# Plain fp32 products instead of three split ones, and value rows summed on VectorE, in a two-stream encoder with gathered experts

## The chip, the cores and the metric

The kernel runs on one core of one Trainium2 chip. The metric is the device time of one launch in microseconds (us): the median of the runs. Beside it stands one profiled execution, whose trace gives every number below that is not a median.

## The reference, cut to what matters

Two requests (`prompt` and `sample`, 256 tokens of 1024 values each) go through the same two layers. Layer 0 mixes tokens by attention, layer 1 by a gated convolution. Each is followed by a retrieval mixer (PEER): per token, 8 heads choose 16 of 16384 experts each, so 128 rows of the table `u` and 128 rows of the table `v`, 4 KB a row.

```python
def peer_block(xc):                      # 128 tokens
    q = (xc @ w_query).reshape(C, 8, 2, 128)
    s = einsum('chpk,hpnk->chpn', q, sub_keys)
    sv, si = top_k(s, 16)                # two lists of 16 keys
    cand = sv[..., 0, :, None] + sv[..., 1, None, :]
    fv, fi = top_k(cand, 16)             # 16 experts of the pairs
    eidx = ...;  g = softmax(fv)
    h = gelu(einsum('chkd,cd->chk', u_tab[eidx], xc))
    return einsum('chk,chkd->cd', g * h, v_tab[eidx])

for i in range(2):
    h = attention(x) if i == 0 else short_conv(x)
    x = layer_norm(ALPHA * x + h, ...)
    x = layer_norm(ALPHA * x + peer(x), ...)
    x = x + sigmoid(x @ ple_w_gate[i]) * (p[i] @ ple_w_proj[i])
```

All inputs are fp32.

## The kernel before, in words

The two requests are two interleaved streams. Stream A (`thread_a`, request 0) does the retrieval sparsely: it gathers the chosen rows. Stream B (`thread_b`, request 1) does it densely: it multiplies all 16384 rows of both tables, two blocks of 128 experts at a time, and weights them with a scattered matrix `G` that is zero where an expert was not chosen. So A's retrieval lives on DMA, GpSimd (POOL) and VectorE (DVE), and B's on TensorE (PE). Each stream is a generator that yields a cost; the next piece is taken from the stream that is behind, and a priority per stage (`pri`) enters the scheduler, which fixes every engine's order at build time. An engine then runs its list strictly in that order.

The stages of A in layer 0: `attention`, layer norm, `route` (the queries and the two top-16 searches, eight rounds of 4 x 128 scores), `peer_gather`, then `ple` (the gated embedding). In layer 1 `conv` stands for `attention`. Stream B has the same stages with `dense_pre` (8 of the 64 pairs of `u` blocks, run ahead into `pre`) and `peer_dense` for the gather.

**Split products.** A weight tile of 128 x 1024 fp32 (512 KB) is loaded by `wload` on SP's queue into `raw` or `ur`; ScalarE (ACT) writes its rounded part `hi`/`uh` as fp32r (L92), and DVE or POOL the rest `lo`/`ul` (L93; `cycle` deals them out in turn). The moving side (`xh`, `xl`, `bx1T0`, `bx1T1`, `ch`, `cl`) is split too. `mm` and `mm_` then issue three fp32r products for each one: high by high, high by low, low by high (L108 to L110, L114 to L117). Only a few matrices go unsplit as plain fp32: the embedding projection (`e.nat`, L106), the scores and values of the attention (L271 to L273, L297), the key scores (L391).

**Gather.** For token tile `t` (of two) `up` gathers the 128 `u` rows of each token one column of indices at a time: one indirect DMA on POOL's queue brings 128 rows, one per token (L486), and one DVE instruction multiplies it with `x[t]` and sums it up (L505). `down` gathers `v` rows by expert position instead: 128 rows of one token sit on 128 partitions, and a stationary matrix `dg` of 128 x 32 that holds coefficients in one column sums them for one token into `av` (L535). Both share the ring `g` of GB = 5 tiles of 512 KB. The order is: all `u` rows of t = 0, then (with `ORDK`) the `v` rows of t = 0 while B routes, then t = 1. A's next stage, `ple`, begins when both tiles are summed and normed.

**Dense.** For a pair of blocks PE runs `dense_u` (2 x 8 products of 256 columns into `hid`), two scatter groups (L638), and `down` (2 x 4 products of 512 columns into the four `out` banks) for the pair before. A pair needs four weight tiles.

Of the kernel before, what the change touches and what calls it, by code (L numbers as in the profile page):

```python
# [11 lines left out]
F32R = mybir.dt.float32r  # L12
# [30 lines left out]
GB = 5  # L43
UR = 4
US = 2
# [3 lines left out]
def encoder_trunk(ctx: ExitStack, tc: tile.TileContext, A: dict):  # L49
# [62 lines left out]
    def mm_(out, a, b, q, first, last):  # L112
        if q == 0:
            nc.tensor.matmul(out, a[0], b[0], start=first, stop=False)  # L114
            nc.tensor.matmul(out, a[0], b[1], start=False, stop=False)  # L115
        else:
            nc.tensor.matmul(out, a[1], b[0], start=False, stop=last)  # L117

    def at(ops, *ix):
        return tuple(o[(slice(None),) + ix] for o in ops)  # L120

    def wblocks(e, name, nb, cols=512):
        kpb = WB // cols
        src = A[name]
        for b in range(src.shape[1]):
            w = wload(e, src[nb, b])
            yield b * kpb, kpb, tuple(z.rearrange("p (c n) -> p c n", n=cols) for z in w)

    def token_major_steps(e, xt, name, nb, ps, kcs=KC):
        ps += [e.mm() for _ in range(NT)]  # L130
        for c0, n, w in wblocks(e, name, nb):
            for t in range(NT):
                for c in range(n):
                    kc = c0 + c
                    mm(ps[t], at(xt, kc, slice(t * P, (t + 1) * P)), at(w, c), kc == 0, kc == kcs - 1)
            yield 2.5
# [7 lines left out]
    def col_major(e, xt, name, cb):  # L144
        ps = e.mm()[:, :S]
        for c0, n, w in wblocks(e, name, cb, cols=P):
            for kc in range(KC):
                mm(ps, at(w, kc), at(xt, kc), kc == 0, kc == KC - 1)
        return ps

    def transpose_x(e, x, xt, natural=False):
        for t in range(NT):
            for half in range(2):
# [4 lines left out]
                if not natural:  # L158
                    o = at(xt, slice(half * 4, half * 4 + 4), slice(t * P, (t + 1) * P))
                    nc.scalar.activation(o[0], pt, AF.Copy)  # L160
                    if len(o) == 2:
                        nc.vector.tensor_sub(o[1], pt, o[0].bitcast(F32))
                else:
                    for j in range(4):
                        o = tuple(z[:, half * 4 + j].rearrange("p (q a b) -> p b a q", q=16, a=4, b=4)[:, 2 * t:2 * t + 2] for z in xt)
                        s = pt[:, j].rearrange("p (b a q) -> p b a q", b=2, a=4, q=16)
                        nc.scalar.activation(o[0], s, AF.Copy)
                        if len(o) == 2:
                            nc.vector.tensor_sub(o[1], s, o[0].bitcast(F32))
# [43 lines left out]
    def attention(e, g, x):  # L213
# [3 lines left out]
        for kb in range(0, KC, 2):  # L217
            raw = e.k2([2 * S])
            nc.scalar.dma_start(raw, A[f"xT{g}"][:, kb * S:(kb + 2) * S])
            split(*(z[:, kb:kb + 2].rearrange("p c s -> p (c s)") for z in xt), raw)  # L220
# [44 lines left out]
        def attend(hp):  # L265
# [20 lines left out]
            def values(hh, t, pr):  # L286
# [11 lines left out]
                nc.scalar.activation(ot[0][:, h, sl], ov[:, :P], AF.Copy)  # L298
                nc.vector.tensor_sub(ot[1][:, h, sl], ov[:, :P], ot[0][:, h, sl].bitcast(F32))
# [34 lines left out]
    def conv(e, x):  # L334
# [10 lines left out]
        for m in range(KC):  # L345
# [17 lines left out]
            else:  # L363
                nc.vector.tensor_mul(cv, cv, ps)
                nc.scalar.activation(po(ht[0][:, m]), nat(cv), AF.Copy)
                nc.vector.tensor_sub(po(ht[1][:, m]), nat(cv), po(ht[0][:, m]).bitcast(F32))
            yield 10
        if bounce:
            ht = e.xt()
            for kb in range(0, KC, 4):  # L370
                raw = e.raw()
                nc.sync.dma_start(raw, hd[:, kb:kb + 4].rearrange("p c s -> p (c s)"))
                split(*(z[:, kb:kb + 4].rearrange("p c s -> p (c s)") for z in ht), raw)
# [3 lines left out]
    def route(e, i, xt, need_t):  # L377
# [73 lines left out]
        if not need_t:  # L451
            eT = T(stp, [P, NT, P], "eT", I32)
            for t in range(NT):
                pt = e.tr([P])
                nc.tensor.transpose(pt, efs[t], ident)
                nc.vector.tensor_copy(eT[:, t], pt)
            return eis, gts, eT
# [31 lines left out]
    def peer_gather(i, x, sel, done):  # L489
        u, v = A[f"u{i}"], A[f"v{i}"]  # L490
        eis, gts, eT = sel
        cT = T(stp, [P, NT, P], "cT")
        cfs = [T(sp, [P, PH, TOPK], "cf", bufs=2) for _ in range(NT)]

        def up(t, heads):
            pri[0] = PG
            ph[0] = True
            yield 0.0
            cf = cfs[t]
            for h in heads:  # L500
                dots = T(sp, [P, TOPK], "dots", bufs=2)
                for k in range(TOPK):
                    c = h * TOPK + k
                    r = gather(u, eis[t][c // 32][:, c % 32:c % 32 + 1])
                    nc.vector.scalar_tensor_tensor(r, r, 1.0, x[t], op0=ALU.mult, op1=ALU.mult, accum_out=dots[:, k:k + 1])  # L505
                    if k % 4 == 3:
                        yield GCOST
                nc.scalar.activation(cf[:, h], dots, AF.Gelu)
                nc.vector.tensor_mul(cf[:, h], cf[:, h], gts[t][:, h])
# [510 lines left out]
```

## Time and profile before

| | us |
|---|---|
| median of 3 runs (4182.75 to 4189.85) | 4186.15 |
| span of the profiled execution, first to last instruction | 4165.6 |
| median less span: the start and end of a launch around it | 20.5 |
| PE busy in the span | 3705.3 (89%) |
| DVE busy | 2680.9 (64%) |
| POOL busy | 2320.6 (56%) |
| ACT busy | 1521.8 (37%) |
| moved by DMA | 1008.36 MB, mean 242 GB/s |

The span is the time from the first to the last instruction of the program on the core; the launch adds some 20 us around it. Busy times overlap, and a share over the whole span is a mean of stages with different limits, so the stages are read one by one. A matmul's duration in the trace includes its way through the array; what a stream of them costs is the distance from start to start.

### The profile page before, as it was taken

What the parts mean: (1) busy time and instruction counts of PE and PEld (TensorE: products, weight loads), DVE (VectorE), ACT (ScalarE), POOL (GpSimd) and SP (SyncE); (2) the same over time, 40 slices, a digit from 0 to 9 for tenths busy, and PEclk for the clock granted to TensorE, in tenths of its full rate; (3) what the DMA queues carried; (4) which work ended last, traced back from release to release, by engine and by line L of the source; (5) the groups of instructions that cost most, each with busy time, mean ns of one, the idle gap of its engine ahead of it and who ended that gap; (6) DMA issues with size and microseconds to landing.
All of it is one profiled execution on the core that took longest, in us unless ns stands there. A gap on an engine that the chain in (4) does not pass through costs nothing. (4 is left out here: it accounts for less than half of the span.)

```text
span 4165.6 us, 61081 instructions
## 1 busy us (share of the span) xinstructions
PE 3705.3 (89%) x22328; PEld 2720.2 (65%) x22328; DVE 2680.9 (64%) x6741; ACT 1521.8 (37%) x2495; POOL 2320.6 (56%) x1927
## 2 busy tenths in 40 slices
PE   8988776899998889999999975769899888999999
PEld 7876564555357776555579864656466777766756
DVE  2348999758459884222255699989843999833325
ACT  4554443434133333222254543234233333433324
POOL 5436777755557665444411255757555776755550
PEclk9999887999999999999999997789999999999999
DMA  6446777876768887666646567777768888877874
GB/s 208 155 133 214 241 258 267 290 266 237 237 231 286 276 281 240 220 215 212 211 147 194 181 228 259 273 272 267 264 231 279 290 291 292 301 267 266 299 248 154
DMA packets 280525, 1008.36 MB, mean 242 GB/s; under 512 B 31648, under 2 KB 33056, under 8 KB 280224
## 3 DMA queue, kind: packets, MB, share of 16 engines
q0 software_dynamic: 147456, 536.94, 36.9%
q1 hardware_dynamic: 124128, 448.85, 32.6%
q10 hardware_dynamic: 8640, 18.68, 1.3%
q8 instruction: 175, 2.87, 0.3%
q14 instruction: 126, 1.03, 0.1%
HBM read 999.09 MB, written 5.24 MB: 241 GB/s over the span
## 5 line engine op out<-in xcount | busy, mean ns | idle before, releaser
L93 POOL TENSOR_TENSOR ul<-ur,uh 128x1024 fp32r<-128x1024 f32 x299 | 747.9, 2501 | 460.3 <-ACT uh L92 435.5
L92 ACT ACTIVATE uh<-ur 128x1024 fp32r<-128x1024 f32 x592 | 625.3, 1056 | 863.3 <-PE hid L109 402.2
L486 POOL DMA_INDIRECT g<-in_v_dram,eT x512 | 515.7, 1007 | 634.0 <-PE av L535 542.3
L486 POOL DMA_INDIRECT g<-in_u_dram,ei x512 | 646.5, 1263 | 367.4 <-DVE g L505 169.4
L505 DVE SCALAR_TENSOR_TENSOR g<-g,xa 128x1024 f32<-128x1024 f32 x512 | 737.1, 1448 | 17.3 <-DMA g<-in_u_dram,ei 17.3
L535 PE MATMUL av<-g,dg 128*32 128x512 f32 x2048 | 713.8, 606 | 27.8 <-POOL dg L529 16.9
L93 DVE TENSOR_TENSOR ul<-ur,uh 128x1024 fp32r<-128x1024 f32 x293 | 371.2, 1267 | 457.8 <-ACT uh L92 436.2
L110 PE MATMUL hid<-bx1T,ul 128*128 128x256 f32 x1792 | 535.0, 299 | 31.0 <-POOL ul L93 24.0
L108 PE MATMUL hid<-bx1T,uh 128*128 128x256 f32 x1792 | 529.6, 296 | 17.8 <-DVE G L640 11.4
L109 PE MATMUL hid<-bx1T,uh 128*128 128x256 f32 x1792 | 521.7, 291 | 0.0
L110 PEld LDWEIGHTS hid<-bx1T,ul 128*128 128x128 f32 x1792 | 355.0, 198 | 79.4 <-issue 37.4
L115 PE MATMUL out<-ul,ch 128*128 128x512 f32 x1024 | 348.9, 413 | 58.7 <-POOL ul L93 38.1
L108 PEld LDWEIGHTS hid<-bx1T,uh 128*128 128x128 f32 x1792 | 355.4, 198 | 50.1 <-ACT uh L92 21.3
L93 DVE TENSOR_TENSOR cl<-hs,ch 128x256 fp32r<-128x256 f32 x224 | 193.2, 865 | 301.9 <-PE out L117 280.3
L535 PEld LDWEIGHTS av<-g,dg 128*32 128x32 f32 x2048 | 140.7, 109 | 351.2 <-issue 264.4
L109 PEld LDWEIGHTS hid<-bx1T,uh 128*128 128x128 f32 x1792 | 354.1, 198 | 12.7 <-issue 10.3
L437 DVE SCALAR_TENSOR_TENSOR junk<-iota,fif,ci 128x54 f32<-128x54 f32 x1024 | 340.3, 376 | 3.0 <-ACT fif L431 2.0
L109 PE MATMUL mm<-lo,xh 128*128 128x512 f32 x640 | 271.1, 424 | 65.9 <-POOL lo L93 36.2
L117 PE MATMUL out<-uh,cl 128*128 128x512 f32 x1024 | 323.0, 396 | 0.4 <-DVE cl L93 0.4
L93 POOL TENSOR_TENSOR lo<-raw,hi 128x1024 fp32r<-128x1024 f32 x88 | 215.4, 2447 | 165.9 <-ACT hi L92 164.0
L114 PE MATMUL out<-uh,ch 128*128 128x512 f32 x1024 | 302.8, 403 | 5.4 <-ACT uh L92 3.2
L638 PE MATMUL hid<-I,J 128*128 128x32 f16 x3584 | 262.6, 232 | 30.8 <-DVE G L640 29.6
(254 smaller groups left out, 6791.8 us busy)
## 6 DMA issues: line engine op xcount, KB each, us to landing
ur<-in_uT_dram SPq DMA_DIRECT2D x256, 512.0 KB, 4.7
ur<-in_v_dram SPq DMA_DIRECT2D x256, 512.0 KB, 4.3
raw<-in_w_qkv_dram SPq DMA_DIRECT2D x144, 512.0 KB, 4.1
raw<-in_w_q_dram SPq DMA_DIRECT2D x32, 512.0 KB, 3.7
ur<-in_w_q_dram SPq DMA_DIRECT2D x32, 512.0 KB, 4.9
raw<-in_c_in_dram SPq DMA_DIRECT2D x24, 512.0 KB, 4.0
ur<-in_c_in_dram SPq DMA_DIRECT2D x24, 512.0 KB, 4.5
raw<-in_w_out_dram SPq DMA_DIRECT2D x16, 512.0 KB, 3.9
```

Source lines behind the costliest of these rows:

```text
L92: nc.scalar.activation(dst_hi, src, AF.Copy)
L93: (eng or nc.vector).tensor_tensor(dst_lo, src, dst_hi.bitcast(F32), op=ALU.subtract)
L108: nc.tensor.matmul(out, a[0], b[0], start=first, stop=False)
L109: nc.tensor.matmul(out, a[0], b[1], start=False, stop=False)
L110: nc.tensor.matmul(out, a[1], b[0], start=False, stop=last)
L114: nc.tensor.matmul(out, a[0], b[0], start=first, stop=False)
L115: nc.tensor.matmul(out, a[0], b[1], start=False, stop=False)
L117: nc.tensor.matmul(out, a[1], b[0], start=False, stop=last)
L437: lk.scalar_tensor_tensor(junk, iota, fif[:, h, k:k + 1], ci[:, h], op0=ALU.is_equal, op1=ALU.mult, accum_out=ef[:, h * TOPK + k:h * TOPK ...
L486: nc.gpsimd.indirect_dma_start(out=t, out_offset=None, in_=tab, in_offset=bass.IndirectOffsetOnAxis(ap=idx, axis=0))
L505: nc.vector.scalar_tensor_tensor(r, r, 1.0, x[t], op0=ALU.mult, op1=ALU.mult, accum_out=dots[:, k:k + 1])
L535: nc.tensor.matmul(acc[n][g * 32:(g + 1) * 32, :], dg[:, g, ri], rows[g][:, n * 512:(n + 1) * 512], start=r == 0, stop=r == 31)
```

## The change

Every product is one plain fp32 matmul straight from the loaded tile: the splits, their `hi` and `lo` rings, the engines that made them and the second halves of the moving tiles are gone. The `v` rows of stream A are gathered like the `u` rows, one index column at a time with one row per token, and DVE multiplies each row by its coefficient and adds it to `acc` (one instruction per gather, the first one a plain multiplication). The heads run one after the other: the `u` rows of head n + 1, then the `v` rows of head n. The rings grow with the room that is free: GB 5 to 8, `ur` 4 to 5, `raw` 3 to 8 in the attention and 2 to 4 behind it.

```diff
-GB = 5
-UR = 4
-US = 2
+GB = 8
+UR = 5
     def wload(e, src, n=WB):
         raw = e.raw()[:, :n]
         nc.sync.dma_start(raw, src)
-        if not e.split:
-            return (raw,)
-        hi, lo = e.hi()[:, :n], e.lo()[:, :n]
-        split(hi, lo, raw, e.sub())
-        return hi, lo
+        return raw
 
     def mm(out, a, b, first, last):
-        if len(a) == 1:
-            nc.tensor.matmul(out, a[0], b[0], start=first, stop=last)
-        else:
-            nc.tensor.matmul(out, a[0], b[0], start=first, stop=False)
-            nc.tensor.matmul(out, a[0], b[1], start=False, stop=False)
-            nc.tensor.matmul(out, a[1], b[0], start=False, stop=last)
+        nc.tensor.matmul(out, a, b, start=first, stop=last)
...
-            for rb in range(32 // RB):
-                dg = T(sp, [P, 4, RB, 32], "dg", bufs=1)
-                nc.gpsimd.memset(dg, 0.0)
-                nc.gpsimd.tensor_copy(dg..., cg[:, :, rb * RB:(rb + 1) * RB])
-                for ri in range(RB):
-                    r = rb * RB + ri
-                    rows = [gather(v, eT[:, t, g * 32 + r:g * 32 + r + 1]) for g in range(4)]
-                    for n in range(2):
-                        for g in range(4):
-                            nc.tensor.matmul(acc[n][g * 32:(g + 1) * 32, :], dg[:, g, ri], rows[g][:, n * 512:(n + 1) * 512], start=r == 0, stop=r == 31)
...
+        def down(t, h):
+            cf = cfs.pop((t, h))
+            if h == 0:
+                acc[t] = T(stp, [P, D], "acc")
+            for k in range(TOPK):
+                r = gather(v, index(t, h * TOPK + k))
+                c = cf[:, k:k + 1]
+                if h == 0 and k == 0:
+                    nc.vector.tensor_scalar(acc[t], r, c, None, op0=ALU.mult)
+                else:
+                    nc.vector.scalar_tensor_tensor(acc[t], r, c, acc[t], op0=ALU.mult, op1=ALU.add)
+                if k % 4 == 3:
+                    yield GCOST
+            if h == PH - 1:
+                nc.vector.scalar_tensor_tensor(x[t], x[t], ALPHA, acc[t], op0=ALU.mult, op1=ALU.add)
+                done(t)
+
+        cfs, acc = {}, {}
+        yield 0.0
+        steps = [(t, h) for t in range(NT) for h in range(PH)]
+        yield from up(*steps[0])
+        for n, step in enumerate(steps):
+            if n + 1 < len(steps):
+                yield from up(*steps[n + 1])
+            yield from down(*step)
...
-                w = wload(e.un if native else e.v, A[f"v{i}"][blk * P:(blk + 1) * P, :])
...
+                w = wload(e, A[f"v{i}"][blk * P:(blk + 1) * P, :])
                 for t in range(NT):
-                    for q in range(1 if native else 2):
...
+                    for n in range(2):
+                        mm(out[t][n], hs[:, b, t * P:(t + 1) * P], w[:, n * 512:(n + 1) * 512], blk == 0, blk == nblk - 1)
...
-    R1 = 3
+    R1 = 8
...
-        w = p2.enter_context(tc.tile_pool(name="w2", bufs=2))
+        w = p2.enter_context(tc.tile_pool(name="w2", bufs=4))
```

PE's list, in the dense retrieval of layer 1 (rows of the kernel before; `hid` is the sum over a pair of `u` blocks, `uh` and `ul` the halves of a `u` tile, `bx1T` the two halves of B's transposed tokens):

```order
19967 L110 MATMUL hid_32473<-bx1T_5023_24763,ul_32477 128x256
19968 L108 MATMUL hid_32473<-bx1T_5023_24763,uh_32476 128x256
19969 L109 MATMUL hid_32473<-bx1T_5024_24764,uh_32476 128x256
19970 L110 MATMUL hid_32473<-bx1T_5023_24763,ul_32477 128x256
19971 L108 MATMUL hid_32473<-bx1T_5023_24763,uh_32476 128x256
19972 L109 MATMUL hid_32473<-bx1T_5024_24764,uh_32476 128x256
```

And PE's list of the change in the dense retrieval of layer 0, where A's gather ends (`out` are the four banks of B's sum, `xa` A's tokens, which `ple` transposes, `ur` the tile as loaded):

```order
3143 L95 MATMUL out_6254<-ur_8811,hs_8808 128x512
3144 L95 MATMUL out_6251<-ur_8817,hs_8808 128x512
3145 L95 MATMUL out_6252<-ur_8817,hs_8808 128x512
3146 L95 MATMUL out_6253<-ur_8817,hs_8808 128x512
3147 L95 MATMUL out_6254<-ur_8817,hs_8808 128x512
3148 L132 MATMUL av_10474<-ident_75,xa_6_99 128x128 x4
3149 L132 MATMUL av_10480<-ident_75,xa_6_99 128x128
3150 L95 MATMUL hid_8787<-bx1T_4352,ur_8788 128x256 x8
3151 L95 MATMUL hid_8787<-bx1T_4352,ur_8798 128x256 x8
```

Three instructions per product have become one, and A's transposes, which read the finished sum of the gather, stand in PE's list after a fifth of the dense pairs of layer 0; the pairs behind them come later in the list. In layer 1 the same transposes of `xa_6` stand at row 7857 of 11572, ahead of all 56 pairs of `u` blocks that are not run ahead.

DVE's list in the gather stage of layer 0, t = 1, before (`ul` and `cl` are low halves) and in the change:

```order
1605 L505 SCALAR_TENSOR_TENSOR g_11665,dots_11661<-g_11665,xa_6_99 128x1024
1606 L93 TENSOR_TENSOR cl_12636<-hs_12626,ch_12635 128x256
1607 L505 SCALAR_TENSOR_TENSOR g_11668,dots_11661<-g_11668,xa_6_99 128x1024
1608 L93 TENSOR_TENSOR cl_12658<-hs_12626,ch_12657 128x256
1609 L640 TENSOR_TENSOR G_12484<-G_12484,hid_12677 128x16x16
1610 L626 TENSOR_TENSOR I_2864_13025<-I_2863_13024,gT_9233 128x1024
1611 L505 SCALAR_TENSOR_TENSOR g_11671,dots_11661<-g_11671,xa_6_99 128x1024
```

```order
1611 L458 SCALAR_TENSOR_TENSOR g_9608,dots_9409<-g_9608,xa_6_99 128x1024
1612 L458 SCALAR_TENSOR_TENSOR g_9611,dots_9409<-g_9611,xa_6_99 128x1024
1613 L521 SCALAR_TENSOR_TENSOR hs_7752<-hs_7752,G_6959 128x512
1614 L476 SCALAR_TENSOR_TENSOR acc_7706<-g_9617,cf_9199,acc_7706 128x1024
1615 L463 TENSOR_TENSOR cf_9614<-cf_9614,gate_390_1481 128x16
1616 L476 SCALAR_TENSOR_TENSOR acc_7706<-g_9620,cf_9199,acc_7706 128x1024
1617 L551 TENSOR_TENSOR I_2051_7870<-I_2050_7869,gT_6214 128x1024
1618 L565 TENSOR_TENSOR G_7658<-G_7658,hid_7665 128x16x16
```

The low halves are gone from DVE, and rows of `v` (L476, each adding to the `acc` of the one before) stand between those of `u` (L458).

## Rows read from the trace of the kernel before

**Rows 1.** The page: the span, and the busy time of each engine.

```profile
span 4165.6 us, 61081 instructions
PE 3705.3 (89%) x22328; PEld 2720.2 (65%) x22328; DVE 2680.9 (64%) x6741; ACT 1521.8 (37%) x2495; POOL 2320.6 (56%) x1927
```

**Rows 2.** The busy time of each engine by stage. Columns: the stretch in us from the start, its length, busy us and instructions of each engine, the granted share of PE's clock, the mean busy share of the DMA engines, GB/s.

```profile
0.00:292.00 292.00, 275.15 (x1344) 227.88 (x1344) 91.05 (x118) 156.81 (x230) 135.54 (x141) 0.99 0.51 168
303.00:816.00 513.00, 386.71 (x1812) 313.21 (x1811) 461.72 (x1388) 213.55 (x369) 386.31 (x349) 0.86 0.73 249
816.00:1043.00 227.00, 216.52 (x1125) 126.74 (x1125) 149.53 (x966) 79.30 (x172) 120.18 (x148) 0.98 0.74 258
1043.00:1571.00 528.00, 465.15 (x3344) 346.70 (x3340) 388.77 (x565) 164.47 (x263) 332.53 (x229) 0.95 0.77 264
1571.00:2097.00 526.00, 522.33 (x2692) 294.37 (x2691) 136.68 (x198) 134.09 (x193) 232.74 (x187) 1.00 0.64 214
...
2522.00:2969.00 447.00, 326.60 (x1840) 255.60 (x1841) 430.89 (x1680) 155.78 (x304) 288.67 (x285) 0.86 0.77 267
...
3214.00:3616.00 402.00, 353.89 (x2596) 301.09 (x2595) 373.46 (x485) 153.30 (x236) 297.01 (x177) 0.98 0.84 293
3616.00:4093.00 477.00, 474.38 (x2944) 322.96 (x2942) 171.81 (x225) 164.14 (x234) 259.25 (x196) 1.00 0.78 265
4093.00:4166.00 73.00, 63.43 (x245) 44.94 (x243) 39.79 (x49) 24.71 (x37) 0.00 (x0) 0.97 0.42 148
```

**Rows 3.** Instructions of single lines with the first and the last start: L211 is the residual add at the end of a mixer (`xa` stream A, `y` and `G` stream B), L539 the one behind A's gather, L670 the one behind B's dense retrieval.

```profile
L211 DVE SCALAR_TENSOR_TENSOR xa<-xa,mm x4: 672/683/687, 279.3 to 291.9; 128x512 f32<-128x512 f32 x4
L211 DVE SCALAR_TENSOR_TENSOR y<-y,mm x4: 671/679/685, 798.9 to 816.2; 128x512 f32<-128x512 f32 x4
L539 DVE SCALAR_TENSOR_TENSOR xa<-xa,av x8: 686/687/689, 1212.7 to 4069.1; 128x512 f32<-128x512 f32 x8
L670 DVE SCALAR_TENSOR_TENSOR G<-G,out x8: 666/676/680, 2522.0 to 4095.3; 128x512 f32<-128x512 f32 x8
```

**Rows 4.** PE in order of time (start, us, line, shape; matmuls in a row are merged): split products of 512 columns, split products of 256 columns, plain fp32 of 256 columns (L271), plain fp32 of 512 columns (L106), scatter products of B's dense retrieval (L638).

```profile
142.01 0.40 PE L108 MATMUL mm<-hi,xh 128*128 128x512 f32 x1
142.25 0.39 PE L109 MATMUL mm<-lo,xh 128*128 128x512 f32 x1
142.48 0.40 PE L110 MATMUL mm<-hi,xl 128*128 128x512 f32 x1
142.71 0.39 PE L108 MATMUL mm<-hi,xh 128*128 128x512 f32 x1
...
3783.37 0.28 PE L108 MATMUL hid<-bx1T,uh 128*128 128x256 f32 x1
3783.49 0.28 PE L109 MATMUL hid<-bx1T,uh 128*128 128x256 f32 x1
3783.60 0.29 PE L110 MATMUL hid<-bx1T,ul 128*128 128x256 f32 x1
3783.73 0.28 PE L108 MATMUL hid<-bx1T,uh 128*128 128x256 f32 x1
...
140.67 0.60 PE L271 MATMUL tr<-qkT 128*128 128x256 f32 x2
141.10 0.38 PE L272 MATMUL tr<-qkT 128*128 128x128 f32 x2
...
2133.64 1.98 PE L106 MATMUL av<-raw,k 128*128 128x512 f32 x4 [0.68 <-ACT k L688]
...
3786.01 0.84 PE L638 MATMUL hid<-I,J 128*128 128x32 f16 x12
3786.78 1.92 PE L535 MATMUL av<-g,dg 128*32 128x512 f32 x8
```

**Rows 5.** The lines L106 and L271: kind and count of their records, duration in ns (least, median, most), first and last start.

```profile
L106 PE MATMUL av<-raw,k x32: 590/592/697, 2133.6 to 4135.5; 128*128 128x512 f32 x32
L271 PE MATMUL tr<-qkT x64: 377/382/636, 63.5 to 791.4; 128*128 128x256 f32 x64
```

**Rows 6.** Groups of instructions: line, engine, operation, out<-in, shapes, count | busy us, mean ns | idle before and who ended it.

```profile
L93 POOL TENSOR_TENSOR ul<-ur,uh 128x1024 fp32r<-128x1024 f32 x299 | 747.9, 2501 | 460.3 <-ACT uh L92 435.5 <-issue 20.2 <-PE hid L638 1.4
L505 DVE SCALAR_TENSOR_TENSOR g<-g,xa 128x1024 f32<-128x1024 f32 x512 | 737.1, 1448 | 17.3 <-DMA g<-in_u_dram,ei 17.3
L535 PE MATMUL av<-g,dg 128*32 128x512 f32 x2048 | 713.8, 606 | 27.8 <-POOL dg L529 16.9 <-DMA g<-in_v_dram,eT 10.6
```

**Rows 7.** DVE and POOL in order of time at one place of layer 1's gather.

```profile
3262.86 3.41 DVE L505 SCALAR_TENSOR_TENSOR g<-g,xa 128x1024 f32<-128x1024 f32 x1
...
3266.54 1.21 DVE L505 SCALAR_TENSOR_TENSOR g<-g,xa 128x1024 f32<-128x1024 f32 x1
3267.68 0.08 DVE L505 DVE_READ_ACCUMULATOR g<-g,xa 128x1 f32 x1
3267.68 1.22 DVE L505 SCALAR_TENSOR_TENSOR g<-g,xa 128x1024 f32<-128x1024 f32 x1
...
3262.17 3.02 POOL L93 TENSOR_TENSOR ul<-ur,uh 128x1024 fp32r<-128x1024 f32 x1 [1.03 <-ACT uh L92]
```

**Rows 8.** The same columns as rows 2, for stretches with gathers of `u` rows and, last, for the 50 us with the densest traffic (`v` gathers and the first loads of a new ring).

```profile
700.00:800.00 100.00, 76.53 (x350) 60.82 (x350) 76.13 (x118) 47.91 (x77) 83.68 (x70) 0.85 0.80 277
...
3300.00:3400.00 100.00, 88.84 (x660) 75.76 (x658) 94.90 (x123) 40.22 (x61) 77.01 (x45) 1.00 0.87 301
3400.00:3500.00 100.00, 84.82 (x624) 72.41 (x624) 98.37 (x118) 35.81 (x56) 65.10 (x43) 1.00 0.84 282
3500.00:3600.00 100.00, 89.64 (x686) 77.91 (x684) 89.94 (x127) 39.30 (x60) 78.81 (x46) 1.00 0.85 307
800.00:850.00 50.00, 40.20 (x145) 19.98 (x144) 26.51 (x38) 11.29 (x22) 29.66 (x25) 0.93 0.94 350
```

**Rows 9.** POOL's gathers of `u` rows (L486) between 700 and 800 us: count, duration in ns (least, median, most), first and last start.

```profile
L486 POOL DMA_INDIRECT g<-in_u_dram,ei x38: 936/1010/1878, 698.7 to 798.7; - x38
```

**Rows 10.** The DMA issues: out<-in, queue, operation, count, median us from issue to landing.

```profile
g<-in_u_dram,ei POOLq DMA_INDIRECT x512, 6.0
g<-in_v_dram,eT POOLq DMA_INDIRECT x512, 5.6
```

More of the change, by code (lines that the diff above doesn't have):

```diff
@@ L126, in wblocks @@
             w = wload(e, src[nb, b])
-            yield b * kpb, kpb, tuple(z.rearrange("p (c n) -> p c n", n=cols) for z in w)
+            yield b * kpb, kpb, w.rearrange("p (c n) -> p c n", n=cols)
     def token_major_steps(e, xt, name, nb, ps, kcs=KC):
@@ L217, in attention @@
         for kb in range(0, KC, 2):
-            raw = e.k2([2 * S])
-            nc.scalar.dma_start(raw, A[f"xT{g}"][:, kb * S:(kb + 2) * S])
-            split(*(z[:, kb:kb + 2].rearrange("p c s -> p (c s)") for z in xt), raw)
+            nc.scalar.dma_start(xt[:, kb:kb + 2].rearrange("p c s -> p (c s)"), A[f"xT{g}"][:, kb * S:(kb + 2) * S])
         if first:
@@ L370, in conv @@
             for kb in range(0, KC, 4):
-                raw = e.raw()
-                nc.sync.dma_start(raw, hd[:, kb:kb + 4].rearrange("p c s -> p (c s)"))
-                split(*(z[:, kb:kb + 4].rearrange("p c s -> p (c s)") for z in ht), raw)
+                nc.sync.dma_start(ht[:, kb:kb + 4], hd[:, kb:kb + 4])
         out_proj(e, x, ht, "c_out")
@@ L451, in route @@
         if not need_t:
[L452 to L457, printed above, removed]
+            return eis, gts
         iT = T(stp, [P, NT, P], "iT", F16)
@@ L490, in peer_gather @@
         u, v = A[f"u{i}"], A[f"v{i}"]
[L491 to L509, printed above, removed]
@@ new lines, in index, with up @@
+        def index(t, c):
+            return eis[t][c // 32][:, c % 32:c % 32 + 1]
+        def up(t, h):
+            dots = T(sp, [P, TOPK], "dots", bufs=2)
+            for k in range(TOPK):
+                r = gather(u, index(t, h * TOPK + k))
+                nc.vector.scalar_tensor_tensor(r, r, 1.0, x[t], op0=ALU.mult, op1=ALU.mult, accum_out=dots[:, k:k + 1])
+                if k % 4 == 3:
+                    yield GCOST
+            cf = T(sp, [P, TOPK], "cf", bufs=2)
+            nc.scalar.activation(cf, dots, AF.Gelu)
+            nc.vector.tensor_mul(cf, cf, gts[t][:, h])
+            cfs[t, h] = cf
@@ L710, in newbx @@
     def newbx():
-        return tuple(T(stp, [P, KC, S], f"bx1T{k}", F32R) for k in range(2))
+        return T(stp, [P, KC, S], "bx1T")
     env = {}
-    SUB1 = "vg"
-    SUBS = ('vgg', 'vg', 'vg', 'vg')
-    NATU = False
     SCU = 1
-    ph = [0]
-    SUBP = 'vg'
     NPRE = 8
@@ L764, in open1 @@
         e.mask = None
-        e.split = True
         e.attn = p1.enter_context(tc.tile_pool(name="attn", bufs=2))
@@ L787, in open2 @@
         a = Env()
-        a.split = True
         a.bounce = True
@@ L791, in open2 @@
         a.pt = lambda: k2([2, S])
-        a.hi = a.lo = ring(gp, [P, D], "g", F32R)
-        a.sub = cycle(SUBA)
         a.raw = a.ln = ring(w, [P, WB], "raw")
-        a.xt = lambda: tuple(T(xp, [P, KC, S], "x", F32R) for _ in range(2))
+        a.xt = a.xt2 = ring(xp, [P, KC, S], "x")
         a.mm, a.tr, a.sc = ring(pav, [P, 512], "av"), psring(pav, "av"), psring(pav, "av")
@@ L799, in open2 @@
         b.deep = PFIRST
-        b.pt = lambda: T(dp, [P, 2, S], "hs", bufs=1)
+        b.pt = lambda: T(dp, [P, 2, S], "hs", bufs=2)
         b.mm, b.tr, b.sc = ring(po, [P, 512], "out"), psring(ph, "hid"), psring(ph, "hid")
-        u = Env()
-        u.split = True
-        u.raw, u.hi, u.lo = ring(dp, [P, WB], "ur", bufs=UR), ring(dp, [P, WB], "uh", F32R, US), ring(dp, [P, WB], "ul", F32R, US)
-        u.sub = phased(cycle(SUBS[0]), cycle(SUBS[2]))
-        v = Env()
-        v.__dict__.update(u.__dict__)
-        v.sub = phased(cycle(SUBS[1]), cycle(SUBS[3]))
-        pe_ = Env()
-        pe_.__dict__.update(u.__dict__)
-        pe_.sub = cycle(SUBP)
-        b.pre = pe_
-        un = Env()
-        un.split, un.raw = False, u.raw
-        b.v, b.un = v, un
-        b.u, b.dense, b.pout, b.phid, b.xp = u, dp, po, ph, xp
-        a.xt2 = a.xt
-        a.nat = Env()
-        a.nat.split, a.nat.raw, a.nat.mm = False, a.raw, a.mm
-        b.split, b.hi, b.lo, b.sub = True, u.hi, u.lo, cycle(SUBB)
-        b.raw = b.ln = u.raw
-        b.xt = lambda: tuple(T(xp, [P, KC, S], "x", F32R) for _ in range(2))
-        def xt2():
-            z = T(dp, [P, 2, KC, S], "G", F32R, bufs=2)
-            return z[:, 0], z[:, 1]
-        b.xt2 = xt2
-        b.nat = un
-        un.mm = b.mm
+        b.dense, b.pout, b.phid, b.xp = dp, po, ph, xp
+        b.raw = b.ln = ring(dp, [P, WB], "ur", bufs=UR)
+        b.xt = ring(xp, [P, KC, S], "x")
+        b.xt2 = ring(dp, [P, KC, S], "G")
         env["a"], env["b"] = a, b
@@ L892, in thread_b @@
                 nc.sync.dma_start(spill[t], x[t])
-            if i == 0 and R2:
+            if i == 0:
                 open2()
@@ L906, in thread_b @@
                 yield cost
-            if i == 0 and not R2:
-                open2()
             e = env["b"]
```

126 lines of the change are left out of this document (21 added, 105 removed).

## The prediction

> **What bounds the kernel now.** The page comes first: PE is busy for 89% of the span, DVE for 64%, POOL for 56% [rows 1]. That mean hides two kinds of stage, so the next view is the busy time by stage, cut at the instructions that end a stage: A's attention ends at 292 us (L211), B's at 816, A's gather of layer 0 at 2097 (t = 1, L539), B's dense retrieval of layer 0 at 2522 and of layer 1 at 4093 (L670), A's second gather at 4069 [rows 3]. In 0 to 292, 1571 to 2097 and 3616 to 4093 PE is busy for 0.94, 0.99 and 0.99 of the time at a granted clock of 0.99 to 1.00: PE sets the pace there. In the gather stages it does not. From 303 to 816 PE is busy for 387 of 513 us and from 2522 to 2969 for 327 of 447, at a granted clock of 0.86, while DVE has 462 and 431 [rows 2]. Closer still, in 3300 to 3500 DVE is busy for 95 and 98 of each 100 us with the DMA engines at 0.87 and 0.84, and in 700 to 800 nothing is full: DVE 76, POOL 84, DMA 0.80 [rows 8]. So the kernel has PE stages, and gather stages in which DVE, POOL and the transfers lie close together. Both ends, A's gather at 4069 and B's at 4095 [rows 3], meet: time saved on one stream alone is not time saved.
>
> **The products.** A product that went as three fp32r matmuls now is one plain fp32 matmul. Starts of split products are 0.23 to 0.24 us apart at 512 columns, 0.12 at 256 [rows 4], so a triple costs 0.69 and 0.36. For plain fp32 the trace has L106 and L271. L271's 32 products in the code (one for each of 8 heads, two token tiles and two streams) left 64 records, and L106's 16 for stream A left 32 [rows 5]: the chip runs two passes for each plain product. A pair of L271's records of 256 columns starts 0.43 us before the next matmul. Four of L106's last 1.98 us together, and the last of them alone at most 0.70 [rows 4, 5], so they start (1.98 - 0.70) / 3 = 0.43 apart. A plain product thus costs 0.86 at 512 and 0.43 at 256 columns, 0.17 and 0.07 **more** than the triple. The Trainium skill, "FP8 and Floating Point Precision", section "TensorE Precision Notes", says that true fp32 goes through the array four times; that rule speaks against trading three passes for it, and by it a product would cost four thirds of the triple, 0.91 for 512 columns where the trace gives 0.86, and the time worked out below would come out near 4390 instead. The sum goes by the trace.
>
> By the order of the change, 1856 products have 512 columns and 2944 have 256. They add 1856 x 0.174 = 323 us and 2944 x 0.073 = 215 us to PE. Against it, the sums of `v` rows leave PE: 2048 instructions, 714 us by their busy time [rows 6]. PE's whole work falls by some 160 to 180 us, but not where PE is the bound: the 714 us lay in gather stages and, for layer 1's t = 1, before 4069.
>
> **PE's order then decides.** A's transposes behind the first gather stand after about a fifth of layer 0's dense products, and behind them come 1040 products of 256 columns, 436 of 512 and 1184 scatters up to the end of dense layer 0. PE waits at the transposes until the gather is summed, then does that block: 1040 x 0.43 + 436 x 0.858 + 1184 x 0.064 (twelve scatters in 0.77 us, [rows 4]) + 12 of small ones = 909 us. At the 0.99 of the two PE stages [rows 2] that is 918. The same happens in layer 1, whose transposes stand ahead of 896 products of 256, 492 of 512 and 1552 scatters: 385 + 422 + 99 = 906, so 915 us, and then a tail like the 73 us of now.
>
> **The gather stages.** What must be moved between the end of A's attention and the transposes is 512 gathers and 188 loads of 0.524 MB, 367 MB. Between the end of dense layer 0 and the second transposes it is 358 gathers (166 of the second 512 fit in before, by DVE's order) and 89 loads, 234 MB. What DVE does in the first: 256 `u` rows at 1.15 (start to start, 1.14 in [rows 7]), 256 `v` rows, 16 rounds of B's and A's routes at no more than 18.7 us (149.5 us for B's eight without gathers, 816 to 1043, [rows 2]), and some 90 of attention, `J` and scatters. A `v` row's instruction is not in the trace. From below it costs what a `u` row does, 1.14; from above the mean of L505 with all its hold-ups, 1.45 [rows 6]. I take 1.25, near the lower end, since it is the same operation without the accumulator's read-out but needs the `acc` of the one before. Sum: 294 + 320 + 299 + 90 = about 1000 us. In the second period 430 + 150 + 60 = 640. What held L505 up goes away: beside POOL's L93 (3.02 us) one took 3.41 where its neighbours take 1.21 [rows 7], and the 299 POOL instructions of L93, 748 us, are gone [rows 6].
>
> So the transfers must tell. Latency of a gather is 6.0 and 5.6 us [rows 10]; eight ring tiles in flight allow 8 x 0.524 MB in 6 us, so the ring no longer sets the pace. What rate holds over hundreds of us with gathers in it? Stages of now have 249 to 293 GB/s [rows 2], and the best 100 us have 307 at a DMA share of 0.85 [rows 8]. From below, the 277 of 700 to 800; from above, the 350 that 50 us with 0.94 reached [rows 8]. I take 307, a rate that was really held beside `u` gathers, loads and a busy PE. The first period is then 367 / 0.307 = 1195 us, the second 234 / 0.307 = 762.
>
> A's attention, before all this, is PE's: 292 + 320 products x 0.174 = 348. The splits of ACT, DVE and POOL leave there too and are counted at nothing; they lie beside PE. **Sum:** 348 + 1195 + 918 + 762 + 915 + 73 = 4211 us of span against 4166; with the 20.5 us of launch 4232, 1.1% over the median, whose profiled execution agrees with it.
>
> **Rivals.** *The transfers are faster, and the gather stages end early.* POOL is free of L93, and where DVE was at 0.95 and 0.98 it, not the DMA engines, set the 301 and 282 GB/s [rows 8]; 307 at a share of 0.85 leaves room. At 350 GB/s the periods would be 1049 and 669, and DVE's 1000 and 640 at 0.94 of the time (the mean of the three windows) 1064 and 681. Sum 348 + 1064 + 918 + 681 + 915 + 73 = 3999, so 4020, 4.0% faster. Against it: no stretch longer than 50 us went so fast. The Trainium skill, "DMA: Bandwidth & Descriptors", section "Specifications", gives a NeuronCore's memory about 358 GB/s; by it the first period could not be under 1025 us. No long run here shows that rate. The point of decision is 1912 us for both periods together, 601 MB, so 314 GB/s: only 2% above the rate I take. *No change* is a rate of 313 to 316.
>
> *The gathers keep the pace of 700 to 800.* There 38 gathers were issued in 100 us [rows 9] with no engine full, so something in turn (a wait for a row, the issue, a tile to come free) takes 2.6 us a gather. If the `u` and `v` rows keep it, 512 take 1347 us and 358 take 942: 348 + 1347 + 918 + 942 + 915 + 73 = 4543, so 4564, 9% slower. Against it: POOL spent much of those 100 us outside of its gathers (38 of about 1.0 us, of 84 busy [rows 8, 9]), and that work goes.
>
> *A plain product is one pass.* Then 512 columns cost 0.43, PE's blocks halve, and the time falls by hundreds of us. The doubled records [rows 5] exclude it.
>
> **How the numbers follow.** The forecast, slower by 0.5 to 4%, has a chance of 0.44; the faster rival with all rates above 316 GB/s 0.37; no change 0.07; the gather pace 0.11; one pass 0.01. About 0.2% is what a measurement of this kernel can tell from no change. The lower bound is 350 GB/s with DVE never in the way, 348 + 1049 + 918 + 669 + 915 + 73 = 3972, so 3990. The upper is 277 GB/s: 348 + 1325 + 918 + 845 + 915 + 73 = 4424, so 4445. The forecast's own range is 4190 to 4400. Faster 0.38, same 0.07, slower 0.55.
>
> **What the profile after would show.** Two records per product on L95, the pairs 0.86 and 0.43 apart. PE idle ahead of L132's transposes of `xa_6`, in both layers, for hundreds of us, with the sum of the gather as releaser. The end of A's first gather near 1543, of dense layer 0 near 2461, of the second gather near 3223. GB/s near 307 in 350 to 1540, DVE under 0.9 there, and waits of DVE for gathered rows. The forecast is wrong if DVE is at 0.95 and its rows arrive early, or if a `v` sum takes much more than 1.25; if the transposes do not wait, PE's work bounds the span and the time is far below.

## The result and the profile after

The changed kernel takes 4089.45 us (median of 4 runs, 4087.1 to 4095.0), the kernel before 4188.0 beside it: a ratio of 0.9764 (95% interval 0.9749 to 0.9779). That is 2.4% **faster**, where 1.1% slower was forecast. 4089 lies between the outer bounds of 3990 and 4445, but below the forecast's own range of 4190 to 4400 and on the wrong side of no change.

The page of the change (span, then busy time of each engine), beside [rows 1]:

```profile
span 4085.7 us, 44452 instructions
PE 3341.1 (82%) x15472; PEld 2231.7 (55%) x15472; DVE 2179.9 (53%) x6430; ACT 589.4 (14%) x1399; POOL 1424.9 (35%) x1476
```

PE has 364 us less busy time than before, but the span falls by 80 only: PE is idle for 745 us where it was for 460. Single lines with their first and last start, beside [rows 3] (L180 is the residual add at a mixer's end, L480 the one behind A's gather, L595 the one behind B's dense retrieval, L426 an integer step near the end of a route):

```profile
L180 DVE SCALAR_TENSOR_TENSOR xa<-xa,mm x4: 670/679/689, 329.9 to 340.9; 128x512 f32<-128x512 f32 x4
...
L480 DVE SCALAR_TENSOR_TENSOR xa<-xa,acc x2: 1211/1218/1225, 1014.8 to 1465.1; 128x1024 f32<-128x1024 f32 x2
L480 DVE SCALAR_TENSOR_TENSOR xa<-xa,acc x4: 1211/1219/1225, 1014.8 to 3128.8; 128x1024 f32<-128x1024 f32 x4
...
L595 DVE SCALAR_TENSOR_TENSOR G<-G,out x8: 670/680/687, 2429.2 to 4037.1; 128x512 f32<-128x512 f32 x8
L426 DVE TENSOR_SCALAR k<-k x4: 216/220/411, 1100.5 to 2975.4; 128x128 int32<-128x128 int32 x4
```

A's attention ends at 341, the first gather at 1465 (its tile t = 0 at 1015), dense layer 0 at 2429, the second gather ends at 3129, dense layer 1 at 4037. Where PE waits in 1000 to 1200, and then in 2700 to 3140 (who waited for whom, us in total, times, longest):

```profile
PE av L132 <- DVE xa L168: 111.7, 1, 111.7
PE hid L432 <- DVE k L431: 60.3, 1, 60.3
PE hid L432 <- DVE k L426: 50.9, 1, 50.9
PE hid L558 <- DVE I L551: 35.6, 1, 35.6
...
PE hid L432 <- DVE k L426: 224.2, 2, 186.0
PE hid L558 <- DVE I L551: 58.0, 6, 33.4
```

L432 are B's transposes at the end of its route, and L558 the first scatter products of B's dense retrieval, which wait for the matrices `I`. PE waits once for the norm of A's tile 0, which follows the sum that ends at 1015. All its other large waits here are for **B's route** and those matrices, whose steps stand in DVE's queue between the row sums; over the whole span L432 waits for 335 us, L558 for 110 on `I`. At the transposes of tile 1, for which the forecast let PE wait, there is no large wait in either layer. In layer 0 PE comes to them at 1491, 26 us after the row above that ends the gather, with work right up to them:

```profile
1484.19 7.10 PE L95 MATMUL out<-ur,hs 128*128 128x512 f32 x16
1491.13 0.71 PE L132 MATMUL av<-ident,xa 128*128 128x128 f32 x5
```

Busy time of each engine by stretch, beside [rows 2] and [rows 8]:

```profile
341.00:1165.00 824.00, 527.61 (x1968) 341.62 (x1968) 714.41 (x2606) 170.43 (x432) 543.95 (x579) 0.82 0.89 325
...
900.00:1200.00 300.00, 31.37 (x194) 25.93 (x192) 286.05 (x862) 24.32 (x72) 230.78 (x196) 0.54 0.88 306
1300.00:2429.00 1129.00, 1098.37 (x5226) 769.90 (x5224) 542.71 (x1644) 143.79 (x347) 287.48 (x300) 0.98 0.69 244
...
2300.00:2400.00 100.00, 100.00 (x354) 65.75 (x352) 67.25 (x83) 5.00 (x10) 57.23 (x50) 1.00 1.03 409
```

From 900 to 1200 PE is busy for 31 us and DVE for 286 of 300. From 1300 to 2429 PE is nearly full (1098 of 1129 us). And 100 us with gathers ran at 409 GB/s, so the 325 of the first gather stage, at a DMA share of 0.89, were not the most that the transfers can do.

### The profile page after: what moved, and what is told of

Its sections match the earlier page's. It is cut to its first block, busy times and chain, and to the rows that moved or that the text cites. A ratio compares the mean times of both kernels' runs of the same rounds, so it can differ in the third digit from the quotient of the medians.

```text
span 4085.7 us, 44452 instructions
## 1 busy us (share of the span) xinstructions
PE 3341.1 (82%) x15472; PEld 2231.7 (55%) x15472; DVE 2179.9 (53%) x6430; ACT 589.4 (14%) x1399; POOL 1424.9 (35%) x1476
## 5 line engine op out<-in xcount | busy, mean ns | idle before, releaser
L95 PE MATMUL hid<-bx1T,ur 128*128 128x256 f32 x3584 | 805.2, 381 | 18.8 <-issue 13.6
L95 PE MATMUL out<-ur,hs 128*128 128x512 f32 x1824 | 812.1, 597 | 5.4 <-DVE G L595 5.4
L95 PEld LDWEIGHTS hid<-bx1T,ur 128*128 128x128 f32 x3584 | 681.7, 191 | 145.0 <-issue 50.3
L444 POOL DMA_INDIRECT g<-in_v_dram,ei x512 | 626.0, 1223 | 339.5 <-issue 97.0
L476 DVE SCALAR_TENSOR_TENSOR acc<-g,cf,acc 128x1024 f32<-128x1024 f32 x508 | 650.9, 1281 | 42.0 <-DMA g<-in_v_dram,ei 36.4
L458 DVE SCALAR_TENSOR_TENSOR g<-g,xa 128x1024 f32<-128x1024 f32 x512 | 618.0, 1226 | 91.1 <-DMA g<-in_u_dram,ei 87.1
L95 PE MATMUL mm<-raw,x 128*128 128x512 f32 x1280 | 570.7, 597 | 9.2 <-DMA x<-in_xT_dram 8.2
L95 PEld LDWEIGHTS out<-ur,hs 128*128 128x128 f32 x1824 | 342.7, 191 | 386.3 <-issue 376.7
L95 PEld LDWEIGHTS mm<-raw,x 128*128 128x128 f32 x1280 | 237.8, 192 | 272.1 <-issue 269.0
L432 PE MATMUL hid<-ident,k 128*128 128x128 f32 x4 | 1.8, 447 | 335.4 <-DVE k L426 275.1
L95 PE MATMUL out<-bx1T,ur 128*128 128x256 f32 x1024 | 235.3, 390 | 14.3 <-DMA ur<-in_w_q_dram 14.3
L563 PEld LDWEIGHTS <-J 128*128 128x128 fp8e4 x3584 | 216.7, 113 | 50.2 <-issue 37.2
L432 PEld LDWEIGHTS hid<-ident,k 128*128 128x128 f32 x4 | 0.7, 183 | 336.9 <-issue 336.9
```

Source lines behind the costliest of these rows:

```text
L95: nc.tensor.matmul(out, a, b, start=first, stop=last)
L432: nc.tensor.transpose(pt[:, k], f, ident)
L444: nc.gpsimd.indirect_dma_start(out=t, out_offset=None, in_=tab, in_offset=bass.IndirectOffsetOnAxis(ap=idx, axis=0))
L476: nc.vector.scalar_tensor_tensor(acc[t], r, c, acc[t], op0=ALU.mult, op1=ALU.add)
L563: nc.tensor.matmul(ps[:, k], J[:, tg * TG + k], I0[:, :, :, k], start=True, stop=True)
```

## The experiments

**What the parts do alone.** `b_vdve` is the kernel before with the change's `peer_gather` put in, nothing else:

```
-    dg = T(...); memset; tensor_copy; nc.tensor.matmul(acc[n][...], dg[:, g, ri], rows[g]...)
+    nc.vector.scalar_tensor_tensor(acc[t], r, c, acc[t], op0=ALU.mult, op1=ALU.add)
```

> The kernel before with one part of the change: the rows of v are summed on DVE, head by head; the split products, POOL's and DVE's low halves and the rings of before stay. Theory 1 (the move of the v rows gives the whole gain, plain fp32 costs 538 us of PE work and gives it back only in part): 3750 to 4000 us, faster than both kernels, since PE's work falls to about 2730 us and the PE stages keep the 0.69 and 0.36 us products. Theory 2 (the splits' work on DVE and POOL is what makes the gather stages long, so the v rows need the change's free POOL): 4150 to 4400 us, no better than before.

4206.6 us, a ratio of 1.0044 (1.0027 to 1.0061): the move alone gains nothing. Its busy times:

```profile
PE 3034.5 (72%) x20272; PEld 2614.6 (62%) x20272; DVE 3337.2 (79%) x7235; ACT 1516.7 (36%) x2488; POOL 2471.6 (59%) x1873
```

Its costliest groups on DVE and POOL (count | busy us, mean ns | idle before):

```profile
L513 DVE SCALAR_TENSOR_TENSOR acc<-g,cf,acc 128x1024 f32<-128x1024 f32 x508 | 723.2, 1424 | 24.9 <-DMA g<-in_v_dram,ei 22.2
L93 DVE TENSOR_TENSOR ul<-ur,uh 128x1024 fp32r<-128x1024 f32 x283 | 384.0, 1357 | 236.7 <-ACT uh L92 234.7 <-DMA raw<-in_c_in_dram 0.5
L93 POOL TENSOR_TENSOR ul<-ur,uh 128x1024 fp32r<-128x1024 f32 x309 | 772.6, 2502 | 720.3 <-ACT uh L92 678.2 <-issue 18.5 <-DMA k<-in_keys_dram 15.2
```

DVE carries the sums and its share of L93, and the sums are stretched: a mean of 1424 ns here, 1281 in the change:

```profile
L476 DVE SCALAR_TENSOR_TENSOR acc<-g,cf,acc 128x1024 f32<-128x1024 f32 x508 | 650.9, 1281 | 42.0 <-DMA g<-in_v_dram,ei 36.4 <-DVE cf L463 0.8 <-DVE acc L476 0.8
```

Theory 1 falls; the outcome is theory 2's.

`b_vdve_nolo` takes the low halves away from that kernel, so that DVE's and POOL's L93 of the weights are gone while the fp32r triples stay. The high half stands in for the low one, so the products come out about doubled, not only less exact, and other rows may be gathered; PE's instructions are as many:

```
-        split(hi, lo, raw, e.sub())
-        return hi, lo
+        nc.scalar.activation(hi, raw, AF.Copy)
+        return hi, hi
```

> The kernel before with the v rows on DVE and without the low halves of the weights (less exact output). With the low halves it was 4207 us, with DVE busy for 79%. If the low halves on DVE and POOL beside the row sums are why the move of the v rows gained nothing there: 3500 to 3750 us. If B's route behind the row sums is enough to hold it, as in the change: 3850 to 4050 us.

3636.2 us (one run), 570 below `b_vdve` and in the first case's range. Its sums take 1282 ns:

```profile
L513 DVE SCALAR_TENSOR_TENSOR acc<-g,cf,acc 128x1024 f32<-128x1024 f32 x508 | 651.2, 1282 | 44.1 <-DMA g<-in_v_dram,ei 40.6 <-issue 0.6
```

`b_nolo` is the same edit to the kernel before itself, with `v` on PE.

> The kernel before without the low halves of the weights: the subtraction is left out and the rounded half is used in its place (the output is less exact); three fp32r products, ACT's rounding, the rings and the v rows on PE stay. If the splits' work on DVE and POOL is what makes the gather stages of before long: 3700 to 3950 us, since PE's work stays at about 3420 us and most of its 740 us of waiting goes. If the long stages come from the gathers themselves (transfers, or DVE's sums of u): 4080 to 4190 us.

3918.2 us (one run), 270 below the kernel before, within the first expectation. So L93 of the weights, with the waits for its result, cost 270 us there and 570 where DVE has both sums.

`a_fp32only` is the plain products alone: the change with the `v` rows back on PE and GB = 5, UR = 4, `raw` 3 and 2.

> The plain fp32 products alone: the rings of before, v rows summed on PE as before. With the big rings this was 4093 us. If the rings matter little: 4090 to 4130 us, so plain fp32 alone gives the whole gain of the change. If they carry part of it: 4140 to 4200 us.

4255.1 us, a ratio of 1.0154 (1.0135 to 1.0173): 1.5% **slower**, more than either expectation. From 3918 to 4255, 337 us, is the price of plain products against triples (less what ACT's rounding and the moving side's halves cost); from 4188 to 3918, 270 us, what the absent L93 gives back. PE's busy time rises from 3652.7 to 4040.4:

```profile
PE 3652.7 (93%) x22328; PEld 2669.9 (68%) x22328; DVE 1717.8 (44%) x6296; ACT 1510.9 (39%) x2496; POOL 1228.0 (31%) x1540
PE 4040.4 (95%) x17528; PEld 2355.1 (55%) x17528; DVE 1565.1 (37%) x5926; ACT 600.2 (14%) x1409; POOL 1271.9 (30%) x1540
```

`a_vpe` adds the big rings to it, `a_vpe_gb5` only those of the weights, `a_rings` is the whole change with the old rings:

```
-GB = 8
-UR = 5
+GB = 5
+UR = 4
-    R1 = 8
+    R1 = 3
-        w = p2.enter_context(tc.tile_pool(name="w2", bufs=4))
+        w = p2.enter_context(tc.tile_pool(name="w2", bufs=2))
```

> The change without one part: v rows are summed on PE with the matrix dg, as before; plain fp32 and the big rings stay. Theory 1 (the gain comes from the v rows leaving PE): 4400 to 4700 us, PE's work is about 3950 us. Theory 2 (the gain comes from POOL and DVE freed of the low halves, and from the rings): 4050 to 4150 us.

> Plain fp32, v rows on PE, big rings of weights (ur 5, raw 8 and 4), but only five tiles for gathered rows. All big rings gave 4093 us, all small ones 4255. If the ring of gathered rows carries the difference (PE takes the v rows four tiles at a time): 4220 to 4260 us. If the weight rings carry it: 4090 to 4130 us.

> The change with the rings of before (GB 5, ur 4, raw 3 and 2). If the rings of gathered rows in flight set the rate of the gather stages (326 to 335 GB/s in the change): 4200 to 4350 us. If five tiles are enough and the rate is that of the transfers or of DVE: 4080 to 4120 us.

`a_vpe` 4093.5 us (0.9778, 0.9758 to 0.9797), `a_vpe_gb5` 4179.2 (0.9981, 0.9971 to 0.9990), `a_rings` 4094.4 (0.9774, 0.9754 to 0.9793). With `v` on PE the rings are worth 162 us, 86 of it by the gather ring and 76 by those of the weights: neither expectation of `a_vpe_gb5` held, the two share it. With `v` on DVE they are worth 5. `a_vpe` came out as its theory 2 and `a_rings` as its second case. So plain products and **either** of the other two parts give some 2.3%, and the third adds 4 or 5 us. The page of `a_vpe` shows why the last step is empty:

```profile
PE 3929.9 (96%) x17528; PEld 2332.1 (57%) x17528; DVE 1564.6 (38%) x5926; ACT 589.0 (14%) x1403; POOL 1289.2 (32%) x1540
```

There PE is full (96%); the change takes 589 us off PE and gets as much idle time (585). Two different limits that end at nearly the same time.

**What holds the gather stages.** `a_halfg` leaves out every second gather and lets two sums read one row, for `u` as below and for `v`, so that DVE's work stays and 268 MB less are moved:

```
+                if k % 2 == 0:
                     r = gather(u, index(t, h * TOPK + k))
```

> The change with every second gather left out (two sums on DVE read the same row, so the output is not the reference's); DVE's work is unchanged, 268 MB less are moved. If the transfers set the gather stages (forecast: 307 GB/s): about 3500 to 3750 us. If DVE sets them: 3950 to 4090 us, DVE busy for over 0.95 from 450 to 1150 us.

4113.9 us (one run): no faster, and 24 above the second expectation. In 500 to 1100 DVE is busy for 575 of 600 us with the DMA engines at 0.70:

```profile
500.00:1100.00 600.00, 384.92 (x1454) 254.63 (x1452) 575.27 (x1749) 135.90 (x322) 303.18 (x299) 0.82 0.70 240
```

The ends of A's first gather (its two tiles), B's route, and PE's largest wait:

```profile
L482 DVE SCALAR_TENSOR_TENSOR xa<-xa,acc x2: 1209/1212/1215, 898.7 to 1283.2; 128x1024 f32<-128x1024 f32 x2
L426 DVE TENSOR_SCALAR k<-k x4: 211/216/222, 1249.7 to 3067.1; 128x128 int32<-128x128 int32 x4
PE hid L432 <- DVE k L426: 500.3, 4, 276.1
```

A's first gather does end earlier, at 1283 instead of 1465, so what is moved (or POOL's issuing, which is halved too) does set a part of its length. But B's route begins to end at 1250 instead of 1100, and PE waits for it 500 us instead of 335.

`a_dve512` does the opposite: all gathers, but DVE sums 512 of the 1024 columns, of `v` as below and of `u`.

```
-  nc.vector.scalar_tensor_tensor(acc[t], r, c, acc[t], ...)
+  nc.vector.scalar_tensor_tensor(acc[t][:, :512], r[:, :512], c, acc[t][:, :512], ...)
```

> The change with DVE summing only 512 of the 1024 columns of each gathered row (the output is not the reference's); every gather and every transfer stays. DVE's work falls by about 600 us. If DVE's queue sets the gather stages (B's route waits behind the sums): 3750 to 3950 us, and the route of layer 0 ends before 1000 us instead of at 1165. If the transfers set them: 4050 to 4100 us.

3643.7 us (one run), 446 less, below even the lower expectation. Its busy times:

```profile
PE 3334.8 (92%) x15472; PEld 2223.3 (61%) x15472; DVE 1649.4 (45%) x6430; ACT 576.9 (16%) x1393; POOL 1189.6 (33%) x1476
```

The ends of A's first gather, and the route's L426, first and last start:

```profile
L480 DVE SCALAR_TENSOR_TENSOR xa<-xa,acc x2: 1216/1220/1225, 998.7 to 1516.2; 128x1024 f32<-128x1024 f32 x2
L426 DVE TENSOR_SCALAR k<-k x4: 212/216/330, 938.7 to 2571.8; 128x128 int32<-128x128 int32 x4
```

PE's two largest waits:

```profile
PE hid L432 <- DVE k L426: 58.5, 3, 31.1
PE hid L432 <- DVE k L431: 51.8, 2, 26.0
```

The busy times from 500 to 1000:

```profile
500.00:1000.00 500.00, 381.59 (x1807) 257.25 (x1805) 373.01 (x1853) 122.56 (x319) 282.72 (x369) 0.87 0.92 339
```

The route begins to end at 939 instead of 1100, PE waits for it 110 us instead of 335, and 339 GB/s are held for 500 us. A's first gather, however, does **not** end earlier: 1516 against 1465. The stretch from the end of A's attention to the end of the gather, in this run and in the change:

```profile
341.00:1516.00 1175.00, 1035.97 (x5051) 690.09 (x5052) 728.70 (x3029) 216.16 (x550) 595.26 (x720) 0.93 0.93 347
341.00:1465.00 1124.00, 768.13 (x3640) 502.38 (x3641) 950.44 (x2940) 198.10 (x500) 727.25 (x720) 0.83 0.90 330
```

DVE is busy for 0.62 of it instead of 0.85, and the DMA engines for 0.93 instead of 0.90. So the two runs part two things. The end of A's gather came 182 us earlier with half the gathers and 51 later with half the sums; the time stayed in the first run and fell by 446 in the second, as B's route came later and earlier. What DVE's work sets in the change is when B's route ends, by what stands in its queue ahead of it. The scheduler builds each kernel's order anew: before the last L426 of layer 0, 359 of A's row sums have started in the change, 510 in `a_halfg`, where the rows come sooner, and 255 in `a_dve512`. So the 446 us are not the shorter sums alone, but also fewer of them ahead of the route.

**A version that beats both.** If the change idles PE and `a_vpe` fills it, the rows should be dealt out: `a_mix` sums the `v` rows of t = 0 on PE with `dg` and those of t = 1 on DVE, with GB = 7.

```
+        for h in range(PH):
+            yield from up(0, h)
+        yield from down_pe(0)
+        yield from up(1, 0)
+        for h in range(PH):
+            if h + 1 < PH:
+                yield from up(1, h + 1)
+            yield from down(1, h)
```

> The change with the v rows of token tile 0 summed on PE (as before) and those of tile 1 on DVE, GB 7. PE's work is about 3600 us, DVE's 320 us less than in the change. If the change is held by DVE's queue while PE idles, and the kernel with all v rows on PE by PE: 3800 to 3980 us, faster than both. If the transfers or B's chain of route steps hold both: 4060 to 4110 us.

3851.0 us, a ratio of 0.9201 (0.9180 to 0.9222), 5.8% below the change and as expected:

```profile
span 3847.2 us, 46104 instructions
PE 3649.5 (95%) x16502; PEld 2275.4 (59%) x16502; DVE 1876.4 (49%) x6180; ACT 594.0 (15%) x1406; POOL 1356.3 (35%) x1508
```

PE has 308 us more work than in the change and 547 less idle time. The order changes with it: tile 0's `v` rows now come behind all of its `u` rows.

**Splits only where DVE is free.** `n_vsplit` is `a_rings` with split products for B's `v` blocks outside A's gather (halves by ACT and DVE, `ph` set around `peer_gather`); `n_mixv` is the same in `a_mix`, which then has room for the small rings only.

```
+                if ph[0]:
+                    ... mm(out[t][n], hs[...], w[...])          # plain
+                    continue
+                for hi, lo, z in ((wh, wl, w), (ch, cl, hs[:, b])):
+                    nc.scalar.activation(hi, z, AF.Copy)
+                    nc.vector.tensor_tensor(lo, z, hi.bitcast(F32), op=ALU.subtract)
```

> The change with the rings of before and with split products (0.69 instead of 0.86 us) for the v blocks of B's dense retrieval while A is not gathering; all else plain fp32. If PE alone sets the time outside of the gather stages: 3930 to 4010 us (some 500 to 900 products of 512 columns at 0.17 us less). If the splits on ACT and DVE or the small rings hold PE up there: 4080 us or more.

> The v rows of token tile 0 on PE and of tile 1 on DVE (3851 us), with the small rings and with split products for the v blocks of B's dense retrieval while A is not gathering. PE was busy for 95% of the span, so if PE's work alone sets the time: 3770 to 3830 us. If the splits or the small rings hold PE up: 3850 us or more.

`n_vsplit` 4042.5 us (0.9660, 0.9637 to 0.9683), 52 below `a_rings` (PE is busy for 71 us less) but between its two expectations: the page counts 496 more PE instructions than in the change, 12 in place of 8 a block, which says that 124 blocks were split, 124 x 4 x 0.174 = 86 us. `n_mixv` 3902.8 (0.9312, 0.9284 to 0.9340), 52 **above** `a_mix`, in its second case. Whether the rings that it gives up or the splits' work on ACT and DVE cost more than the splits save is not shown: no run of `a_mix` has the small rings alone.

## Why the prediction was wrong

By its own terms, forecast and then measured, in us: A's attention 348, 341; to the end of the first gather 1195, 1124; PE's block to the end of dense layer 0 918, 964; to the end of the second gather 762, 700; dense layer 1 915, 908; tail 73, 49; around the span 20.5, 1.8. The errors are -7, -71, +46, -62, -7, -24 and -19, together -144: 4232 against 4088 (the profiled execution took 4087.5).

- **"PE waits at the transposes until the gather is summed", then does its block, is the step that failed**, and with it the rival's 4020, which went the same way. PE's waits lie earlier, at tile 0's norm (112 us, the one wait for a sum of the gather) and B's route (111 and 224 us). Where the forecast let PE wait until 1543, it came to the transposes at 1491 with work right up to them: the block began 26 us behind the gather's end and has 28 us of idle time (in 1990 to 2429) where 9 were allowed for, so it is 46 us longer than forecast. The time does not follow the gather's end: with that end 182 us earlier it did not fall (`a_halfg`), with it 51 us later it fell by 446 (`a_dve512`), and with it 118 us later, at 1583, it rose by 5 (`a_rings`). The order shows where each instruction stands, but the forecast let only one queue wait, for its last input. The route's steps behind row sums in DVE's queue were the wait to price.
- **"So the transfers must tell ... I take 307"** was mis-sized, and the two gather terms are 133 us too long by it: 367 MB in 1124 us are 326 GB/s, 234 in 700 are 334. Where 301 and 282 GB/s were read, DVE was at 0.95 and 0.98 [rows 8], so these were not known to be the transfers' own rates. The first rival had the rate on the right side. That the transfers have a part in the gather's length stands (`a_halfg`). DVE's about 1000 us of work in the first period were 950, and it waited for gathered rows for 52 us only. That the sum of all terms came within 3.5% owes something to luck: the gather's end and PE's own arrival happened to lie close together in both layers.
- **The products were priced right.** Records of the change, in order of time (merged by shape):

```profile
3510.48 1.98 PE L563 MATMUL hid<-I,J 128*128 128x32 f16 x32
3512.29 7.10 PE L95 MATMUL out<-ur,hs 128*128 128x512 f32 x16
3519.23 7.07 PE L95 MATMUL hid<-bx1T,ur 128*128 128x256 f32 x32
3526.13 1.98 PE L563 MATMUL hid<-I,J 128*128 128x32 f16 x32
```

Sixteen records, eight products of 512 columns, take 6.94 us to the next start: 0.87 each; 32 of 256 take 6.90, so 0.43. The dense term of layer 1 was off by 7 us. The Trainium skill, "FP8 and Floating Point Precision", section "TensorE Precision Notes", would have 0.91 by four passes, an estimate from the triple; this trace stays with 0.87.
- **What the gain paid for was under-rated.** Taking L93 off DVE and POOL was said to let the rows go, and then counted at nothing, since the transfers were to set the pace. `b_nolo` prices it at 270 us. The fp32 products then cost 337 of the 538 us added to PE, and the rings or the move of `v` give back 166: 4188 - 270 + 337 - 166 = 4089. Before, the sums beside POOL's L93 were stretched [rows 6, 7]; in the change L458 has a mean of 1226 ns where L505 had 1448. In the trace of before, the 117 sums of L505 that overlap an L93 of POOL in time have a mean of 2205 ns, the other 395 of 1224. The Trainium skill, "SBUF — State Buffer", section "Who interferes with whom", has a DVE instruction with two SBUF inputs contend with a GpSimd instruction that reads SBUF, through a port pair that one of them holds exclusively; these means agree, and so do `b_vdve` and `b_vdve_nolo` (1424 and 1282 ns for the same sum).
- **The price of a `v` sum** was 1.25 and is 1.28: three in a row, 1353.73 to the next instruction at 1357.57.

```profile
1353.73 3.92 DVE L476 SCALAR_TENSOR_TENSOR acc<-g,cf,acc 128x1024 f32<-128x1024 f32 x3
1357.57 1.22 DVE L458 SCALAR_TENSOR_TENSOR g<-g,xa 128x1024 f32<-128x1024 f32 x1
```

- **The 20.5 us around the span** were no cost of a launch: the profiled execution of the change took 1.8 us more than its span. All executions on record last about 2 us longer than their span, so the profiled one of before, with a span of 4165.6, was some 18 us shorter than the median, and shorter than any timed one (4179 at the least).

Open: why the rings of weights are worth 76 us with `v` on PE; PE is idle for 46 us less with them, but no single wait ends. For the ring of gathered rows the traces say where its 86 us lie: PE's busy time in the `v` products is 669 us with GB = 5, with either rings of weights, and 580 with GB = 8, for the same 2048 instructions. Why they pack closer is open too.

## What to carry to other kernels

A transfer rate read where another engine is at 0.95 may be that engine's rate: test which one is full before it becomes a bound. When a stage is made shorter, look at its end and at the total: here the long stage ended 182 us earlier and nothing was gained. In an in-order queue look for the short chain that a busy neighbour waits for, here B's route behind A's row sums; that wait, 335 of 745 us, was the largest part of TensorE's idle time. When two placements of one job end at the same time with different engines full, split the job: half of the `v` rows on each took another 5.8% off.

## What was not expected of the hardware

Gathers and loads together reached 409 GB/s over 100 us (DMA share 1.03) at 2300 in the change, against 350 in the densest 50 us of before [rows 8]. The Trainium skill, "DMA: Bandwidth & Descriptors", section "Specifications", has about 358 GB/s for a NeuronCore's memory; here, with one core running, more was measured, so that figure did not bound this kernel.
